# A pad of 224 bytes, GpSimd's order written out, and the first down operands loaded ahead, in a one-layer hybrid decoder block

## The chip, the cores and the metric

The kernel runs on one core of one Trainium2 chip. The metric is the device time of one execution in microseconds (us). Beside it stands the span of one profiled execution, from its first to its last instruction. The engines are TensorE (PE: matmuls and transposes; PEld: its weight loads), VectorE (DVE), ScalarE (ACT) and GpSimd (POOL); SP (SyncE) only issues the DMAs, in its own order.

## The reference

One layer over 1024 tokens of width 1024, in float32, cut to what matters here:

```python
h = rmsnorm(x, g_attn); proj = h @ w_in            # two mixers read it
mix = concat(dilated_attention(...), diff_attention(...))
x = x + mix @ w_out                                # (1024,1024) @ (1024,1024)
h = rmsnorm(x, g_ffn)
gate, up = split(h @ w_gate_up, 2)                 # 2 x 2816 columns
x = x + (silu(gate) * up) @ w_down                 # 2816 rows
return rmsnorm(x, g_final)
```

## The kernel before

Every float32 operand of a matmul is split in a high part (a cast to the matmul type, by ScalarE) and a low part (the rest, by GpSimd or VectorE); a product is then three matmuls: high by high, high by low, low by high. `split` (L684 to 687) makes such a pair, `split_weights` (L125) that of a weight tile of 1024 columns. One matmul is 128x128 by 128x512.

The stages follow each other: input projections and attention; the out projection, whose first three quarters (`op` in the profile) run among the attention heads, and whose last quarter (`op_l`, L626, rows 2 and 3 of the mixers' tiles) comes after them; the second norm; gate and up; down; the last norm.

**Around the last out projection.** Eight token tiles t go in the order 0, 2, 4, 6, 1, 3, 5, 7. For each there are two groups of six matmuls (n = 0, 1), added to `x1[t]` by VectorE (L628), and then `norm` (L153): ScalarE squares and sums (L157), VectorE scales the sum (L141), GpSimd raises it to the power -1/2 (`nst_f`, L143), and two halves of `hn_f` are written: by VectorE (L165), or, for the second half of tiles 0, 2, 4 and 6, by ScalarE (L162) and GpSimd (L163). `flip_low(j)` transposes the two halves of tile 2j on PE (`tp_b`, L846, two PSUM buffers with the tag T), and ScalarE and VectorE write them as high and low parts of the operands `h` (L848, L849). `flip_high(j)` does so for tile 2j+1 and for a difference `t` (L865). `others(j)` (L873 to 875, GpSimd) forms three more differences in place.

**Gate and up.** For pairs p = 0 to 10 of 128 columns each of gate and up is a matrix of 2x2 blocks. For p = 0 eight plain block products are used (`gate_up_first`), whose left operands `ops` are split from `raw_g` and `raw_u` (L687); for the others, seven products of sums of blocks (`pa`, `pb`, `pc`, `pd` in the profile, 12 matmuls each, L747). `store_act` splits the block results into `ao` and stores them in DRAM as `act_d[p]`.

**Down.** The seven products are run over pairs of p: `oa` (from `act_d`, L951) by `wd` (from `raw_d`, L956, differences formed by GpSimd at L968 to 974), in the order 1, 5, 6, 7, 2, 3, 4, each 24 matmuls (`d`, L1015), summed in `acc`. Three of `acc` start as `x1` read back from DRAM (`acc<-x_d`). The last p is done by plain products (`dl`, L1051), followed by the last norm (L1054 to 1067).

**What sets the order.** A scheduler orders each engine's instructions by a model of their costs; in the stretch from the last out projection to the first products of p = 1, a `manual_schedule` block keeps PE's instructions in the order of the code. All DMAs go through SP, one after the other in SP's order; each also waits until the eighth DMA before it has landed. Tiles come from pools of a fixed number of buffers, and a tile's first writer waits for the last reader of the buffer before it: `raw` one buffer, `w` four, `x1t` eight, `mix` four, `oa` ten. The operands `wd` go in turn through eight buffers that the operands `wg` and `wu` used before them. The pools of one side share one stack: the pad `end_pad` lies under all tiles of the right side (`hT`, `x1`, `mix`, `mid`).

The place of the last out weights before, and the loads of the first down operands:

```python
wo = [out_weights(2, n) for n in range(2)]                    # L877, pool "w", raw buffer shared
...
for i in ORDER:                                               # down, first pair
    oa = [load_act(p, i) for p in pair]                       # pool "down", memory of the tiles h
```

Of the kernel before, what the change touches and what calls it, by code (L numbers as in the profile page):

```python
# [71 lines left out]
def tile_hybrid_block(  # L72
# [21 lines left out]
    wp = ctx.enter_context(tc.tile_pool(name="weights", bufs=2))  # L94

    ep = ctx.enter_context(tc.tile_pool(name="end", bufs=1, side="right"))
    ep.tile([P, 24], F32, name="end_pad")
    dp = ctx.enter_context(tc.tile_pool(name="scratch", bufs=1, space=DRAM))
    pp = ctx.enter_context(tc.tile_pool(name="psum", bufs=2, space=PSUM))

# [19 lines left out]
        return bass.AP(tensor=ap1d.tensor, offset=ap1d.offset, ap=[[0, P], [1, n]])  # L120


    def split_weights(src, a, name, tag="w", eng=None):

        small = tag == "w"  # L125
        pool = wp if small else mapp
        raw = pool.tile([P, 1024], F32, tag="raw" if small else "KL", bufs=1 if small else 2, name=f"raw_{name}")
        nc.sync.dma_start(raw.rearrange("p (a b) -> p a b", a=a), src)
        if small:
            w = [pool.tile([P, 1024], F32R, tag=tag, bufs=4, name=f"w_{name}_{i}") for i in "hl"]  # L130
        else:
            both = pool.tile([P, 2, 1024], F32R, tag=tag, name=f"w_{name}")
            w = [both[:, i, :] for i in range(2)]
        nc.scalar.copy(w[0], raw)
        (eng or nc.gpsimd).tensor_tensor(w[1], raw, w[0].bitcast(F32), op=ALU.subtract)
        return [w_.rearrange("p (a b) -> p a b", a=a) for w_ in w]
# [145 lines left out]
    def run_all(gen):  # L282
        for _ in gen:
            pass
# [342 lines left out]
                i += 1  # L627
        nc.vector.tensor_tensor(x1[t][:, cols], ps, x1[t][:, cols], op=ALU.add)  # L628

    def out_weights(k0, n):  # L630
        return split_weights(w_out_v[:, k0 : k0 + 2, n * 512 : (n + 1) * 512], 2, f"o{k0}_{n}")

    def out_proj(k0, first=False):
        mix = mix_tiles(k0)
# [32 lines left out]
    def h2_tile(i):  # L667
        hB[i] = h2p.tile([P, 2, 4, 512], F32R, tag=f"h{i}", name=f"h2_{i}")

    for i in (1, 6, 7, 5, 2, 4, 3):  # L670
        if i in (4, 6):
            ops0[i == 4] = h2p.tile([P, 4, 2, 512], F32R, tag=f"h{i}", name=f"ops0_{i}")
        else:
            h2_tile(i)
# [148 lines left out]
    def store_act(p, c):  # L823
# [14 lines left out]
        for i, op in ops.items():  # L838
            nc.sync.dma_start(act_d[p][i - 1], op.bitcast(F32))

    def flip(src, i, j, name):

        cols = slice(j * P, (j + 1) * P)
        ps = psum("T", f"tp_{name}")
        for k in range(4):
            nc.tensor.transpose(ps[:, k * P : (k + 1) * P], src[:, k * P : (k + 1) * P], ident)  # L846
        pv = ps.rearrange("p (a b) -> p a b", a=4)
        nc.scalar.copy(hB[i][:, 0, :, cols], pv)  # L848
        nc.vector.tensor_tensor(  # L849
            hB[i][:, 1, :, cols], pv, hB[i][:, 0, :, cols].bitcast(F32), op=ALU.subtract  # L850
        )
# [22 lines left out]
        g.tensor_tensor(v[:, LO], u[:, LO], v[:, LO], op=ALU.add)  # L874
        g.tensor_tensor(v[:, HI], v[:, HI], v[:, LO], op=ALU.subtract)

    wo = [out_weights(2, n) for n in range(2)]  # L877
    mix = mix_tiles(2)
    load_mix(mix, 2, 0)
    gf = mid.tile([P, D], F32, tag="gf", bufs=1, name="gf")  # L880
    nc.sync.dma_start(gf, broadcast(g_ffn[0], D))
    load_mix(mix, 2, 1)
    raw0 = [load_raw(0, up) for up in range(2)]
    with tc.manual_schedule(engines={mybir.EngineType.PE}):
        for i, t in enumerate(TOKENS):
            for n in range(2):
                out_proj_group(mix, wo[n], t, n, "l")
            high = xp.tile([P, D], F32, tag="x1t", name=f"hn_f{t}") if t % 2 else None
            hns[t] = norm(mid, x1[t], gf, t, "f", high)
            nc.sync.dma_start(x1_d[t], x1[t])  # L890
            if 2 <= i < 6:
                flip_low(i - 2)
        a0 = [[], []]
        for up in range(2):
            for i in range(4):
                a0[up].append(as_left(ops0[up][:, i]))
                split(raw0[up][i], a0[up][i], nc.gpsimd)
        c0 = [block_tile(0, up) for up in range(2)]
        first = [gate_up_first(up, a0[up], c0[up], c0[0] if up else None) for up in range(2)]
        flip_high(0)  # L900
        for i in range(8):
            next(first[i // 4])
            if i % 2 == 0 and i < 6:
                flip_high(1 + i // 2)
        w1 = [gate_up_weights(1, 0)]
        for j in range(4):
            others(j)
        for i in range(4):
            next(first[0])
            flip(hns[2 * i + 1][:, LO], 7, i, f"t3_{i}")  # L910
        h2_tile(6)
        w1.append(gate_up_weights(1, 1))
        for i in range(4):
            next(first[1])
            flip(hns[2 * i][:, LO], 6, i, f"t2_{i}")
        h2_tile(4)
        store_act(0, c0[1])
        gate = block_tile(1, 0)
        steps = gate_up(1, 0, w1[0], BANK_SETS[0], gate)
        for i in range(4):  # L920
            next(steps)
            flip(hns[2 * i][:, HI], 4, i, f"t4_{i}")
        for _ in steps:
            pass
    for p in range(1, NPAIR):
        for up in range(2):
            if p == 1 and not up:
                continue
            w_ = w1[1] if p == 1 else gate_up_weights(p, up)
            c = block_tile(p, up)  # L930
            run_all(gate_up(p, up, w_, BANK_SETS[up], c, gate if up else None))
            if up:
                store_act(p, c)
            else:
                gate = c
# [9 lines left out]
    def next_bank(name):  # L945
        n_ps[0] += 1
        return psum(CYCLE[n_ps[0] % 8], name)

    def load_act(p, i):
        op = dn.tile([P, 2, 512], F32R, tag="oa", bufs=10, name=f"oa_{p}_{i}")  # L950
        nc.sync.dma_start(op.bitcast(F32), act_d[p][i - 1])  # L951
        return op

    def raw_down(p):
        raw = mxp.tile([P, 2, D], F32, tag="mix", name=f"raw_d{p}")
# [34 lines left out]
    for c0 in range(0, NPAIR - 1, 2):  # L990
        pair = (c0, c0 + 1)
        last = c0 == NPAIR - 3
        raws = [raw_down(p) for p in pair]
        for i in ORDER:
            oa = [load_act(p, i) for p in pair]
            if c0 == 0:
                if i == 5:
                    load_x1(7, 1, 1)
                    load_x1(4, 1, 0)
                    for tq in range(4):  # L1000
                        g.tensor_tensor(acc[4][:, tq], acc[4][:, tq], acc[7][:, tq], op=ALU.subtract)
                elif i == 7:
                    load_x1(2, 0, 0)
                elif i == 2:
                    load_x1(3, 0, 1)
                elif i == 3:
                    nc.sync.dma_start(gfin, broadcast(g_final, D))
            wd = [right_operand(blocks, i, p) for blocks, p in zip(raws, pair)]
            for tq in range(4):
                ps = next_bank(f"d{c0}_{i}_{tq}")  # L1010
                sl = slice(tq * P, (tq + 1) * P)
                n = 0
                for a, w in zip(oa, wd):
                    for l_, r_ in ((0, 0), (0, 1), (1, 0)):
                        mm(ps, a[:, l_, sl], w[:, r_, :], start=n == 0, stop=n == 5)  # L1015
                        n += 1
                if c0 == 0 and i in (1, 5, 6):
                    nc.scalar.copy(acc[i][:, tq], ps)
                else:
                    v.tensor_tensor(acc[i][:, tq], ps, acc[i][:, tq], op=ALU.add)  # L1020
            if last:
                if i == 6:
                    combine(v, 6, 1, 6)
                elif i == 7:
                    combine(v, 7, 6, 7)
                    combine(g, 6, 6, 5)
                    combine(v, 5, 7, 5)
                elif i == 2:
                    combine(g, 2, 1, 2)
                elif i == 3:  # L1030
                    combine(g, 3, 6, 3)
                elif i == 4:
                    combine(v, 4, 7, 4)
    raw = raw_down(NPAIR - 1)
    wl = []
    for i, src in enumerate(raw):
        wl.append(ring(f"wd{NPAIR - 1}_{i}"))
        split(src, wl[i], nc.gpsimd)
    oal = [load_act(NPAIR - 1, i + 1) for i in range(4)]
    for m, rows in ((0, (2, 3)), (1, (4, 5))):  # L1040
        for tq in range(4):
            sl = slice(tq * P, (tq + 1) * P)
            t = 2 * tq + m
            y = xp.tile([P, D], F32, tag="x1t", name=f"y_{t}")
            for n, r in enumerate(rows):
                ps = next_bank(f"dl_{t}_{n}")
                i = 0
                for k in range(2):
                    a, w = oal[2 * m + k], wl[2 * k + n]
                    for l_, r_ in ((0, 0), (0, 1), (1, 0)):  # L1050
                        mm(ps, a[:, l_, sl], w[:, r_, :], start=i == 0, stop=i == 5)  # L1051
                        i += 1
                v.tensor_tensor(y[:, n * 512 : (n + 1) * 512], ps, acc[r][:, tq], op=ALU.add)
            st = dn.tile([P, 2], F32, tag="fst", bufs=8, name=f"fst_{t}")  # L1054
            junk = mxp.tile([P, D], F32, tag="mix", name=f"sq_{t}")
            nc.scalar.activation(junk, y, AF.Square, accum_out=st[:, 0:1])
            rms_power(st, EPS, True)
            for n in range(2):
                cols = slice(n * 512, (n + 1) * 512)
# [30 lines left out]
```

## Time and profile before

| | us |
|---|---|
| median of three runs | 1272.24 |
| lowest, highest | 1271.81, 1273.27 |
| the profiled execution | 1273.28 |
| its span | 1271.5 |
| PE busy in the span | 1232.7 |
| VectorE, GpSimd, ScalarE busy | 782.0, 737.3, 578.7 |

The span is 1.8 us shorter than the profiled execution, which is 1.0 us above the median. A row of the waits reads: who waited, at which line, for whom; then the total, the number of waits and the longest. A row of the timeline reads: start, duration, engine, line, operation, output and inputs, sizes, number of instructions merged, and in brackets the idle time before it with what ended it. A row of the windows gives the stretch, then the busy time of each engine with the number of its instructions, then the clock granted to PE, the share of the DMA engines in use, and GB/s.

### The profile page before, as it was taken

The numbers are of one execution on the slowest core, as the hardware profiler recorded it, in microseconds if no ns is written. First come the engines' busy times: TensorE is split into PE (matmuls) and PEld (weight loads), VectorE is DVE, ScalarE is ACT, GpSimd is POOL, SyncE is SP. The second block draws the span as 40 slices with busy tenths as digits, with TensorE's granted clock in tenths as the row PEclk, the third lists the DMA queues.
The fourth block names the chain that finished last, engine by engine and source line by source line (L and its number), as shares of the span: only waits on it lengthen the run. The fifth ranks groups of instructions, "written<-read, shape, count | busy, mean of one in ns | idle before, by whom it ended". The sixth has DMA issues, their size and how long they took to land.

```text
span 1271.5 us, 18475 instructions
## 1 busy us (share of the span) xinstructions
PE 1232.7 (97%) x6318; PEld 1040.1 (82%) x6318; DVE 782.0 (62%) x1666; ACT 578.7 (46%) x1298; POOL 737.3 (58%) x664
## 2 busy tenths in 40 slices
PE   6999999999999999988999999999999989999997
PEld 5989989988998888867888888888888867888885
DVE  6558678876765687748555454553555543655587
ACT  5446566665765665435433334343444343222214
POOL 2024434454443444346645887878978895756676
PEclk8999999999999999998999999999999999999999
DMA  6232133123213472252332354424445359956633
GB/s 216 64 91 76 51 100 92 43 86 98 92 51 92 149 291 100 84 177 96 116 116 83 116 182 166 168 98 144 154 166 182 132 199 410 399 202 246 216 131 132
DMA packets 99613, 184.63 MB, mean 145 GB/s; under 512 B 6920, under 2 KB 58376, under 8 KB 99520
## 3 DMA queue, kind: packets, MB, share of 16 engines
q1 hardware_dynamic: 99520, 183.46, 41.6%
q8 instruction: 50, 0.82, 0.3%
q14 instruction: 43, 0.35, 0.1%
HBM read 119.41 MB, written 55.63 MB: 138 GB/s over the span
## 4 chain that ended last, share of the span: by engine, by line
PE 85%; DMA 5%; DVE 5%; POOL 2%; ACT 1%; issue 1%; SPq 0%; DVEq 0%; POOLq 0%; ACTq 0%
PE d L1015 11%; PE pa_u L747 5%; PE op L626 5%; PE pa_g L747 5%; PE pd_g L747 4%; PE pc_g L747 4%; PE pc_u L747 4%; PE pd_u L747 4%; PE vpsa L221 4%; PE ppsqa L248 4%; PE ppsqd L248 4%; PE ppskd L248 3%; PE ppska L248 3%; PE pb_g L747 3%; PE pb_u L747 3%; PE vpsd L221 3%
## 5 line engine op out<-in xcount | busy, mean ns | idle before, releaser
L1015 PE MATMUL d<-wd,oa 128*128 128x512 f32 x840 | 197.4, 396 | 6.3 <-DMA oa<-act_d 6.3
L1015 PEld LDWEIGHTS d<-wd,oa 128*128 128x128 f32 x840 | 158.2, 189 | 45.4 <-ACT wd L686 5.2
L1020 DVE TENSOR_TENSOR acc<-d,acc 128x512 f32<-128x512 f32 x128 | 87.2, 688 | 68.7 <-PE d L1015 68.6
L545 POOL TENSOR_SCALAR t_a<-t_a,st_a 128x384 f32<-128x384 f32 (+2 forms) x96 | 55.6, 590 | 105.9 <-DVE st_a L441 75.2
L687 POOL TENSOR_TENSOR wd<-raw_d,wd 128x512 fp32r<-128x512 f32 x54 | 73.4, 1380 | 69.4 <-ACT wd L686 66.9
L686 ACT CAST wd<-raw_d 128x512 fp32r<-128x512 f32 x74 | 45.3, 620 | 148.1 <-PE d L1015 95.0
L687 POOL TENSOR_TENSOR ao<-act,ao 128x512 fp32r<-128x512 f32 x52 | 74.7, 1445 | 47.8 <-ACT ao L686 47.5
L687 POOL TENSOR_TENSOR wu<-raw_u,wu 128x512 fp32r<-128x512 f32 x50 | 69.2, 1401 | 29.3 <-DMA act_d<-ao 18.6
L686 ACT CAST wg<-raw_g 128x512 fp32r<-128x512 f32 x70 | 42.1, 619 | 92.1 <-POOL raw_g L700 36.1
L687 POOL TENSOR_TENSOR wg<-raw_g,wg 128x512 fp32r<-128x512 f32 x50 | 74.8, 1513 | 5.3 <-ACT wg L686 2.9
L686 ACT CAST wu<-raw_u 128x512 fp32r<-128x512 f32 x70 | 40.7, 619 | 68.7 <-DMA raw_u<-in_w_gate_up 27.2
L431 ACT ACTIVATE t_d<-t_d,st_d 128x384 f32<-128x384 f32 (+3 forms) x96 | 58.5, 613 | 14.6 <-DVE st_d L418 14.1
L456 ACT CAST ath_a<-tp_a 128x384 fp32r<-128x384 f32 (+2 forms) x96 | 45.1, 479 | 42.8 <-PE tp_a L450 41.7
L431 ACT ACTIVATE t_a<-t_a,st_a 128x384 f32<-128x384 f32 (+2 forms) x96 | 58.7, 613 | 12.5 <-DVE st_a L418 11.7
L747 PE MATMUL pc_u<-h,wu 128*128 128x512 f32 x240 | 60.5, 395 | 0.0
L747 PE MATMUL pc_g<-h,wg 128*128 128x512 f32 x240 | 59.9, 391 | 0.0
L747 PE MATMUL pa_g<-h,wg 128*128 128x512 f32 x240 | 59.5, 393 | 0.3 <-ACT gate L773 0.3
L747 PE MATMUL pa_u<-h,wu 128*128 128x512 f32 x240 | 59.5, 393 | 0.0
L747 PE MATMUL pd_u<-h,wu 128*128 128x512 f32 x240 | 59.2, 392 | 0.0
L747 PE MATMUL pd_g<-h,wg 128*128 128x512 f32 x240 | 58.6, 393 | 0.0
L503 POOL TENSOR_SCALAR t_d<-t_d,st_d 128x384 f32<-128x384 f32 (+3 forms) x48 | 30.0, 634 | 47.0 <-DVE st_d L441 32.5
L686 ACT CAST ao<-act 128x512 fp32r<-128x512 f32 x74 | 42.4, 618 | 30.8 <-DVE act L760 11.4
(266 smaller groups left out, 3579.4 us busy)
## 6 DMA issues: line engine op xcount, KB each, us to landing
act_d<-ao SPq DMA_DIRECT2D x74, 512.0 KB, 3.4
oa<-act_d SPq DMA_DIRECT2D x74, 512.0 KB, 4.7
raw_g<-in_w_gate_up SPq DMA_DIRECT2D x11, 1024.0 KB, 6.2
raw_u<-in_w_gate_up SPq DMA_DIRECT2D x11, 1024.0 KB, 6.0
raw_d<-in_w_down SPq DMA_DIRECT2D x11, 1024.0 KB, 7.4
strip<-gtab SPq DMA_DIRECT2D x12, 512.0 KB, 3.7
xt<-in_x SPq DMA_DIRECT2D x8, 512.0 KB, 5.2
raw_o<-in_w_out SPq DMA_DIRECT2D x8, 512.0 KB, 3.9
```

The lines of the kernel that those rows point to most:

```text
L221: mm(ps[:, :256], l_, r_, start=n == 0, stop=n == 3 * KT - 1)
L248: mm(ps, l_[:, k, :], r_[:, k, sl], start=i == 0, stop=i == 3 * KT - 1)
L431: nc.scalar.activation(tt[:, :n], tt[:, :n], AF.Exp, bias=st[:, last : last + 1], scale=-1.0, accum_out=st[:, 2 + c : 3 + c],)
L456: nc.scalar.copy(hi, pv)
L503: nc.gpsimd.tensor_scalar(t0[:, :n], t0[:, :n], s0[:, 4:5], 1.0, op0=ALU.mult, op1=ALU.mult)
L545: nc.gpsimd.tensor_scalar(t0[:, :n], t0[:, :n], s0[:, 4:5], 1.0, op0=ALU.mult, op1=ALU.mult)
L626: mm(ps, l_[:, k, sl], r_[:, k, :], start=i == 0, stop=i == 5)
L686: nc.scalar.copy(dst[:, 0], src)
L687: eng.tensor_tensor(dst[:, 1], src, dst[:, 0].bitcast(F32), op=ALU.subtract)
L747: mm(ps, a[:, l_, k, :], b[:, r_, k, :], start=start and i == 0, stop=i == 11, skip_group_check=not start,)
L1015: mm(ps, a[:, l_, sl], w[:, r_, :], start=n == 0, stop=n == 5)
L1020: v.tensor_tensor(acc[i][:, tq], ps, acc[i][:, tq], op=ALU.add)
```

## The change

Five things are edited. The pad under the right side's tiles grows from 24 to 56 floats (224 bytes). The second half of the last out weights, high and low, goes into a tile `wo_l1` in the place of the operand tile `h7` instead of two `w` buffers, and the tile `h7` proper is made later. In the stretch of the last out projection GpSimd's instructions too keep the order of the code, and there the splits of the first gate operands stand behind the norms of tiles 6, 1, 3 and 5, those of the up operands behind all. Four loads of `act_d` (products 1 and 5 of p = 0 and 1) are made ahead of the last up block, into `x1t` buffers instead of the down stage's own. In the last norm the squares of the last tile are summed in two halves.

```diff
-    ep.tile([P, 24], F32, name="end_pad")
+    ep.tile([P, 56], F32, name="end_pad")
...
-        if small:
+        if parts:
+            w = parts
+        elif small:
             w = [pool.tile([P, 1024], F32R, tag=tag, bufs=4, name=f"w_{name}_{i}") for i in "hl"]
...
+    wo_l1 = None
     for i in (1, 6, 7, 5, 2, 4, 3):
-        if i in (4, 6):
+        if i == 7:
+            wo_l1 = h2p.tile([P, 4, 1024], F32R, tag=f"h{i}", name="wo_l1")
+        elif i in (4, 6):
...
+    def load_act(p, i, pool, tag, bufs):
+        op = pool.tile([P, 2, 512], F32R, tag=tag, bufs=bufs, name=f"oa_{p}_{i}")
+        nc.sync.dma_start(op.bitcast(F32), act_d[p][i - 1])
+        return op
...
-    wo = [out_weights(2, n) for n in range(2)]
+    wo = [out_weights(2, 0), out_weights(2, 1, [wo_l1[:, i] for i in range(2)])]
...
-    with tc.manual_schedule(engines={mybir.EngineType.PE}):
+    a0 = [[as_left(ops0[up][:, i]) for i in range(4)] for up in range(2)]
+    with tc.manual_schedule(engines={mybir.EngineType.PE, mybir.EngineType.Pool}):
         for i, t in enumerate(TOKENS):
...
             if 2 <= i < 6:
                 flip_low(i - 2)
-        a0 = [[], []]
-        for up in range(2):
-            for i in range(4):
-                a0[up].append(as_left(ops0[up][:, i]))
-                split(raw0[up][i], a0[up][i], nc.gpsimd)
+            if i >= 3 and i < 7:
+                split(raw0[0][i - 3], a0[0][i - 3], nc.gpsimd)
+        for i in range(4):
+            split(raw0[1][i], a0[1][i], nc.gpsimd)
+    with tc.manual_schedule(engines={mybir.EngineType.PE}):
...
+        h2_tile(7)
         w1 = [gate_up_weights(1, 0)]
...
             c = block_tile(p, up)
+            if up and p == NPAIR - 1:
+                early = {(q, i): load_act(q, i, xp, "x1t", 8) for i in (1, 5) for q in range(2)}
             run_all(gate_up(p, up, w_, BANK_SETS[up], c, gate if up else None))
...
-            oa = [load_act(p, i) for p in pair]
+            oa = [early.get((p, i)) or load_act(p, i, dn, "oa", 10) for p in pair]
...
+            halves = t == KT - 1
...
+                if halves:
+                    nc.scalar.activation(junk[:, cols], y[:, cols], AF.Square, accum_out=st[:, n : n + 1])
+            if halves:
+                v.tensor_tensor(st[:, 0:1], st[:, 0:1], st[:, 1:2], op=ALU.add)
+            else:
+                nc.scalar.activation(junk, y, AF.Square, accum_out=st[:, 0:1])
```

The order that comes of it differs in three places; up to the last out projection all engines keep theirs.

**First place: the norms after the last out projection.** GpSimd before, from the low part of the last out weights on (`nst_f` is the power, `hn_f` with `gf` the second half of a normalised tile, `ops_6` and `ops_4` the first gate and up operands):

```order
L135 TENSOR_TENSOR w_o_1_l<-raw_o_1_6913,w_o_1_h 128x1024
L687 TENSOR_TENSOR ops_6_6826<-raw_g_6927,ops_6_6826 128x512 x4
L143 TENSOR_TENSOR nst_f_6949<-nst_f_6949,nhalf 128x1
L687 TENSOR_TENSOR ops_4_6830<-raw_u_6929,ops_4_6830 128x512 x4
L143 TENSOR_TENSOR nst_f_6974<-nst_f_6974,nhalf 128x1
L163 TENSOR_TENSOR hn_f_6950<-hn_f_6950,gf 128x512
```

GpSimd now, from tile 6's second half on (the rows ahead of it are the powers and second halves of tiles 0, 2 and 4; L883 and L884 are `others`):

```order
L165 TENSOR_TENSOR hn_f_7037<-hn_f_7037,gf 128x512
L692 TENSOR_TENSOR ops_6_6826<-raw_g_6925,ops_6_6826 128x512
L145 TENSOR_TENSOR nst_f_7078<-nst_f_7078,nhalf 128x1
L692 TENSOR_TENSOR ops_6_6826<-raw_g_6925,ops_6_6826 128x512
L883 TENSOR_TENSOR hn_f_7077<-hn_f_7077 128x512
L884 TENSOR_TENSOR hn_f_6948<-hn_f_7077,hn_f_6948 128x512
L145 TENSOR_TENSOR nst_f_7118<-nst_f_7118,nhalf 128x1
L692 TENSOR_TENSOR ops_6_6826<-raw_g_6925,ops_6_6826 128x512
```

The eight splits that stood ahead of the first second half stand behind four of them, among the powers of the odd tiles and `others`.

**Second place: ScalarE in the same stretch.** ScalarE now, from the high part of the last out weights on (L159 squares, L164 scales a second half, L858 writes a high part of `h`):

```order
L136 CAST wo_l_6827<-raw_o_1_6913 128x1024
L159 ACTIVATE hn_f_6948,nst_f_6947<-x_0_5584 128x1024
L691 CAST ops_6_6826<-raw_g_6925 128x512 x3
L164 ACTIVATE hn_f_6948<-x_0_5584,nst_f_6947 128x512
L691 CAST ops_6_6826<-raw_g_6925 128x512
L159 ACTIVATE hn_f_6973,nst_f_6972<-x_2_5586 128x1024
L691 CAST ops_4_6830<-raw_u_6927 128x512 x4
L858 CAST h_1_6825<-tp_b_0_7006 128x4x128
L159 ACTIVATE hn_f_6998,nst_f_6997<-x_4_5588 128x1024
L858 CAST h_2_6829<-tp_b_0_7013 128x4x128
L164 ACTIVATE hn_f_6973<-x_2_5586,nst_f_6972 128x512
```

The casts of `ops` still stand among the first norms; before, all eight of them stood ahead of the first scaling (L162) and the first square stood behind four of them.

**Third place: the start of the down stage.** PE now, from the fifth product of the last up block on:

```order
L752 MATMUL pd_u_10387<-h_5_6828,wu_5_10316 128x512 x10
L1024 MATMUL d_1_0_10468<-wd_1_10462,oa_1_10324 128x512 x3
L1024 MATMUL d_1_1_10476<-wd_1_10462,oa_1_10324 128x512 x3
L1024 MATMUL d_1_0_10468<-wd_1_10465,oa_1_10326 128x512
L1024 MATMUL d_1_1_10476<-wd_1_10465,oa_1_10326 128x512
L1024 MATMUL d_1_2_10484<-wd_1_10462,oa_1_10324 128x512 x3
L1024 MATMUL d_1_2_10484<-wd_1_10465,oa_1_10326 128x512
L1024 MATMUL d_5_2_10530<-wd_5_10507,oa_5_10328 128x512
L1024 MATMUL d_1_3_10492<-wd_1_10462,oa_1_10324 128x512 x3
L752 MATMUL pc_u_10373<-h_4_7606,wu_4_10304 128x512 x12
L752 MATMUL pd_u_10387<-h_3_6831,wu_3_10320 128x512 x12
L1024 MATMUL d_1_0_10468<-wd_1_10465,oa_1_10326 128x512 x2
```

Before, the two products `pc_u` and `pd_u` of 12 followed the ten directly, and all matmuls `d` came behind them; now 16 matmuls `d` stand ahead of the two. SP's queue there now:

```order
L844 DMA act_d_3_6899<-ao_4_10144 128x1024
L848 DMA oa_1_10324<-act_d_0_6833 128x1024
L848 DMA oa_1_10326<-act_d_0_6840 128x1024
L848 DMA oa_5_10328<-act_d_4_6837 128x1024
L848 DMA oa_5_10330<-act_d_4_6844 128x1024
L844 DMA act_d_5_6901<-ao_6_10150 128x1024
L844 DMA act_d_4_6900<-ao_5_10156 128x1024
```

The four loads stood behind the first store of the last block (`act_d_0<-ao_0`) before, and now stand some ten DMAs earlier. Behind that store now come two loads of `acc`, the second store (`act_d_1<-ao_1`), and only then `oa_6`.

More of the change, by code (lines that the diff above doesn't have):

```diff
@@ L120, in broadcast, with split_weights @@
         return bass.AP(tensor=ap1d.tensor, offset=ap1d.offset, ap=[[0, P], [1, n]])
-    def split_weights(src, a, name, tag="w", eng=None):
+    def split_weights(src, a, name, tag="w", eng=None, parts=None):
         small = tag == "w"
@@ L628, in out_proj_group, with out_weights @@
         nc.vector.tensor_tensor(x1[t][:, cols], ps, x1[t][:, cols], op=ALU.add)
-    def out_weights(k0, n):
-        return split_weights(w_out_v[:, k0 : k0 + 2, n * 512 : (n + 1) * 512], 2, f"o{k0}_{n}")
+    def out_weights(k0, n, parts=None):
+        return split_weights(w_out_v[:, k0 : k0 + 2, n * 512 : (n + 1) * 512], 2, f"o{k0}_{n}", parts=parts)
     def out_proj(k0, first=False):
@@ L947, in next_bank @@
         return psum(CYCLE[n_ps[0] % 8], name)
[L949 to L952, printed above, removed]
     def raw_down(p):
@@ L1038, in tile_hybrid_block @@
         split(src, wl[i], nc.gpsimd)
-    oal = [load_act(NPAIR - 1, i + 1) for i in range(4)]
+    oal = [load_act(NPAIR - 1, i + 1, dn, "oa", 10) for i in range(4)]
     for m, rows in ((0, (2, 3)), (1, (4, 5))):
@@ L1044, in tile_hybrid_block @@
             y = xp.tile([P, D], F32, tag="x1t", name=f"y_{t}")
+            st = dn.tile([P, 2], F32, tag="fst", bufs=8, name=f"fst_{t}")
+            junk = mxp.tile([P, D], F32, tag="mix", name=f"sq_{t}")
+            halves = t == KT - 1
             for n, r in enumerate(rows):
@@ L1052, in tile_hybrid_block @@
                         i += 1
[L1053 to L1056, printed above, removed]
+                cols = slice(n * 512, (n + 1) * 512)
+                v.tensor_tensor(y[:, cols], ps, acc[r][:, tq], op=ALU.add)
+                if halves:
[4 more added lines that the diff above has]
+                nc.scalar.activation(junk, y, AF.Square, accum_out=st[:, 0:1])
             rms_power(st, EPS, True)
```

## The prediction

> **What bounds the kernel now.** I read the page's first lines, then the table of PE's waits, then windows of PE's clock, then the timelines of all engines at the two places where PE stands still.
>
> ```profile
> span 1271.5 us, 18475 instructions
> PE 1232.7 (97%) x6318; PEld 1040.1 (82%) x6318; DVE 782.0 (62%) x1666; ACT 578.7 (46%) x1298; POOL 737.3 (58%) x664
> ...
> PE d L1015 <- DMA oa<-act_d: 6.3, 4, 3.4
> ...
> PE tp_b L846 <- POOL hn_f L163: 4.6, 1, 4.6
> PE op_l L626 <- POOL w_o_l L135: 1.9, 1, 1.9
> PE tp_b L846 <- DVE hn_f L165: 1.4, 1, 1.4
> PE op_l L626 <- ACT w_o_h L134: 0.9, 1, 0.9
> ...
> 560.00:562.00 2.00, 2.00 (x5) 1.58 (x6) 0.00 (x0) 0.28 (x1) 0.00 (x0) 0.56 1.05 351
> ...
> 576.00:578.00 2.00, 2.00 (x7) 1.61 (x6) 1.87 (x2) 1.19 (x2) 2.00 (x3) 0.50 0.00 0
> ...
> 700.00:760.00 60.00, 60.00 (x263) 49.05 (x262) 27.83 (x35) 22.73 (x41) 51.65 (x38) 1.00 0.43 156
> ...
> 1042.00:1044.00 2.00, 2.00 (x7) 1.51 (x6) 2.00 (x2) 0.00 (x0) 2.00 (x2) 0.50 0.99 270
> ```
>
> PE is the bound: 1232.7 of 1271.5 us, and in the gate and up blocks 60 of every 60, with GpSimd at 52. So a wait taken from PE ahead of those blocks is time saved, unless it comes back later. The waits that the change touches are the four at the last out projection (8.8 us) and those for `oa` (6.3). After such waits PE also runs at a granted clock of 0.5 for some microseconds, so that seven matmuls fill 2 us in two of these windows.
>
> By the Trainium skill, "TensorE: Matmul & The Clock Gate", section "What's actually happening", the clock falls to half after at least one idle window of about 3.4 us. The level agrees with the 0.50 here, the length less so: the first slow window follows waits of 0.9 and 1.9 with one matmul between them.
>
> **The last out projection.** PE's six matmuls of tile 0, second half, wait for the weights; then its transposes wait for the first norm.
>
> ```profile
> 545.56 0.38 SPq L128 DMA_DIRECT2D raw_o<-in_w_out  x1
> ...
> raw_o<-in_w_out SPq DMA_DIRECT2D x8, 512.0 KB, 3.9
> ...
> 556.44 1.04 ACT L134 CAST w_o_h<-raw_o 128x1024 fp32r<-128x1024 f32 x1 [10.56 <-PE op L626]
> 561.72 2.18 ACT L686 CAST ops<-raw_g 128x512 fp32r<-128x512 f32 x4 [4.24 <-DMA raw_g<-in_w_gate_up]
> 565.80 2.18 ACT L686 CAST ops<-raw_u 128x512 fp32r<-128x512 f32 x4 [0.84 <-DMA raw_u<-in_w_gate_up]
> 576.13 0.72 ACT L162 ACTIVATE hn_f<-x,nst_f 128x512 f32<-128x512 f32 x1 [1.47 <-POOL nst_f L143]
> ...
> 557.56 2.35 POOL L135 TENSOR_TENSOR w_o_l<-raw_o,w_o_h 128x1024 fp32r<-128x1024 f32 x1 [9.89 <-ACT w_o_h L134]
> 562.42 5.07 POOL L687 TENSOR_TENSOR ops<-raw_g,ops 128x512 fp32r<-128x512 f32 x4 [2.51 <-ACT ops L686]
> 573.87 1.26 POOL L163 TENSOR_TENSOR hn_f<-hn_f,gf 128x512 f32<-128x512 f32 x1
> ...
> 589.13 1.41 DVE L165 SCALAR_TENSOR_TENSOR hn_f<-x,nst_f,gf 128x512 f32<-128x512 f32 x2
> 594.19 3.00 DVE L165 SCALAR_TENSOR_TENSOR hn_f<-x,nst_f,gf 128x512 f32<-128x512 f32 x2
> ...
> 599.11 0.66 PE L846 MATMUL tp_b<-ident,hn_f 128*128 128x128 f32 x4 [0.56 <-DVE h L849]
> ...
> 605.86 0.44 PE tp_b L846 x4
> ```
>
> The weights' place: the raw half is asked for at 545.6 and takes 3.9, yet its cast stands idle 10.56 us until PE has left the `w` buffer at 556.4. In `wo_l1` it can run at 549.5, the low part is there by 549.5 + 1.0 + 2.4 = 552.9, and PE comes at 556.4. Both waits go: 2.8 us. The cover is 3.5 us; without it they come back one for one.
>
> The norms: PE needs 0.234 us a matmul (96 of them take 22.5 us in a row quoted below), 1.4 a group of six, and 0.44 for four transposes. From 556.4 it does five groups (tiles 0, 2, 4) and is at the first transposes at 563.4. The power no longer stands behind the splits. But the new order of ScalarE keeps three casts of `ops` ahead of tile 0's scaling, and `raw_g` lands at 561.7: 561.7 + 3 x 0.55 + 0.72 + GpSimd's 1.26 = 565.4. PE does the first four transposes and waits 1.6. Tile 6's twelve matmuls end at 568.7. For tile 2 ScalarE has the four up casts ahead, which end at 565.8 + 2.2 = 568.0, then two writes of `h` (0.6 each, as the casts below, 1.14 for two), a square (1.04 in the last norm's row), a scaling (0.72): 571.0, and GpSimd's 1.26 make 572.2; without the transposes' 0.44 PE has stood 3.1 more. After tile 1 the same queue holds both PSUM buffers of the transposes once more; I take 1.7 us, between the two waits worked out. Tiles 3, 5 and 7 and the transposes between them (3 x 2.8 + 2 x 0.9, with tile 1's 2.8) then bring PE to the first `flip_high` at 572.6 + 2.8 + 0.9 + 2.8 + 0.9 + 1.7 + 5.6 = 587.3, and with some 2 us of half clock at 589.3.
>
> The eight splits do not vanish: at 1.27 each (5.07 for four) they lie where VectorE writes the odd tiles' norms. Two of these take 1.41 us at 589.1 and 3.00 at 594.2; the second pair ran beside GpSimd. The Trainium skill, "SBUF — State Buffer", section "Who interferes with whom", says a VectorE instruction with two SBUF inputs and a GpSimd one that reads SBUF block each other; that speaks against the change, and the two rows agree with it.
>
> In the new order the power of tile 3 stands behind a split and two steps of `others`, which wait for the difference that VectorE forms from tile 1. From VectorE's turn to tile 1 (about 581) I count 3.0 for the pair, 0.7 for `x1`, 0.7 for the difference, 2 x 1.3 on GpSimd, 0.6 the power: 588.6; then what lay between 594.2 and 599.1 before, 4.9: the second `flip_high` is ready near 593.5, and PE's own pace gives 589.3 + 0.9 + 2.8 = 593.0. Contention that hits the difference too would add 1.1. I take 594.1 against 599.1: **5.0 us** gained. From both sides: 2.8 if only the weights' waits go, and 8.2 if VectorE and the clock hold nothing back (587.3 + 3.7 = 591.0).
>
> **The start of the down stage.** PE stops when the last up block is done.
>
> ```profile
> 1031.51 2.95 PE L747 MATMUL pc_u<-h,wu 128*128 128x512 f32 x12
> ...
> 1040.70 4.57 PE L1015 MATMUL d<-wd,oa 128*128 128x512 f32 x12 [3.44 <-DMA oa<-act_d]
> ...
> 1054.96 22.52 PE L1015 MATMUL d<-wd,oa 128*128 128x512 f32 x96 [0.30 <-DMA oa<-act_d]
> 1079.25 11.10 PE L1015 MATMUL d<-wd,oa 128*128 128x512 f32 x47 [1.77 <-DMA oa<-act_d]
> ...
> 1025.24 0.38 SPq L956 DMA_DIRECT2D raw_d<-in_w_down  x1
> ...
> 1030.98 1.14 ACT L686 CAST wd<-raw_d 128x512 fp32r<-128x512 f32 x2 [7.35 <-DMA raw_d<-in_w_down]
> ...
> 1037.59 1.27 POOL L970 TENSOR_TENSOR raw_d<-raw_d 128x512 f32<-128x512 f32 x1
> ...
> 1035.23 1.26 DVE L760 TENSOR_TENSOR act<-act,gate 128x512 f32<-128x512 f32 x1
> 1038.83 1.80 DVE L687 TENSOR_TENSOR ao<-act,ao 128x512 fp32r<-128x512 f32 x1 [2.35 <-ACT ao L686]
> ...
> oa<-act_d SPq DMA_DIRECT2D x74, 512.0 KB, 4.7
> ...
> L1020 DVE TENSOR_TENSOR acc<-d,acc 128x512 f32<-128x512 f32 x128 | 87.2, 688 | 68.7 <-PE d L1015 68.6
> ```
>
> With products 1 and 5 loaded ahead, PE goes on at 1031.5 with 16 matmuls `d`. Their high parts need the second `raw_d`: asked for at 1025.2, cast at 1031.0 to 1032.1, while PE reaches them at 1032.9: 0.8 to 1.3 us of cover, and every microsecond beyond stops PE with `pc_u` and `pd_u` behind. Then these 24 (5.6), then the other 32 of products 1 and 5 (7.5): 1031.5 + 3.7 + 5.6 + 7.5 = 1048.3, where before product 6 began at 1055.0.
>
> A new wait stands there. `oa_6` is behind the store of `ao_1` in SP's queue. `ao_1` comes from `pc_u`, now done at 1040.8 - 2.8 = 1038.0, and VectorE first writes the low part of `wd_7`, whose cast is third in ScalarE's row behind GpSimd's difference (1037.6 + 1.3 = 1038.9, then 2 x 0.6: 1040.1). Then 1.8 for it (as `ao` in its row), 0.7 for the addition of `pc_u` (688 ns for its kind), 1.26, a cast 0.6, 1.80 for `ao_1`: 1046.3; two issues (0.3) and 4.7 to land: 1051.3. PE waits 3.0 us. The gain at product 6 is 1055.0 - 1051.3 = 3.7. The half clock I charge at 0.9, half of what the twelve matmuls at 1040.7 lost (4.6 instead of 2.8), as I can't tell whether this wait brings it on.
>
> The later wait of 1.77 I take as gone: product 4's `oa` now stands ahead of two `raw_d`, and 2 MB less are asked for in that stretch. Sum: 3.7 - 0.9 + 1.7 = **4.5 us**. Bounds: 8.4 if `oa_6` is in time (1055.0 - 1048.3 + 1.7); nothing if `oa_6` takes 8.8, the page's 4.7 and 4.1 more of queueing. By the page of the clock gate in the Trainium skill a wait of 3.0 us could stay under one window, and the sum would be 5.4.
>
> The early loads themselves: four issues on SP behind `ao_4`'s store, in the pause before the next `ao` is ready; hidden by PE's blocks, where the DMA share is 0.43.
>
> **The last norm and the pad.**
>
> ```profile
> 1265.13 1.04 ACT L1056 ACTIVATE sq<-y 128x1024 f32<-128x1024 f32 x1
> ...
> 1265.30 1.27 POOL L1062 TENSOR_TENSOR y<-y,gfin 128x512 f32<-128x512 f32 x1 [0.83 <-ACT y L1061]
> 1266.53 0.55 POOL L143 TENSOR_TENSOR fst<-fst,nhalf 128x1 f32<-128x1 f32 x1
> ...
> L1015 PE MATMUL d<-wd,oa 128*128 128x512 f32 x840 | 197.4, 396 | 6.3 <-DMA oa<-act_d 6.3
> L747 PE MATMUL pc_g<-h,wg 128*128 128x512 f32 x240 | 59.9, 391 | 0.0
> ```
>
> The square of the last tile gets shorter, but the power behind it waits for GpSimd's product of the tile before (1265.3 + 1.27), which is not moved: I take 0; at most half the square, 0.5, either way. The pad moves the right side's tiles by 128 bytes. No row shows what an address costs; the nearest are matmuls of one shape on tiles at different places, 391 and 396 ns, 1.3% apart, or 16 us of PE's 1233 either way as the far bounds. Nothing gives the shift a sign, so I take 0.
>
> **Sum.** 5.0 + 4.5 = 9.5 us. The profiled execution would go from 1273.3 (span 1271.5 to 1262.0) to 1263.8; it is 1.0 above the median, so the median from 1272.2 to **1262.7 us**.
>
> **The rivals.** (A) The forecast, 5.5 to 13.5 us gained, 1258.7 to 1266.7: 0.70. For it: no PE wait in the blocks between. (B) One of the two places gives nothing: the splits keep VectorE as late as before, or `oa_6` takes over the whole wait; 4.5 to 5 us gained, about 1267.5. For it: VectorE is busy throughout around 594; against it: it stood still at 560, waiting for the same weights. 0.13. (C) The gain comes back: GpSimd, now behind by eight splits, holds up the blocks' weights. It is at 52 of 60 there and can win back 8 us in 60, so I believe this little; no change, 1272: 0.05. (D) Slower: the pad makes PE's right-side operands dearer. It decides from 9.5 of 1233, 0.8% a matmul; at 1.3% the time is 1262.7 + 16 = 1278.7: 0.04. (E) Both upper bounds, 16.6 gained, 1255.6: 0.08. For it: the waits that I put in place of the old ones are worked out from orders alone.
>
> The range 1257.0 to 1268.5 holds nearly all of A, B's most and a little of E, some 0.82. What a measurement tells from no change is 0.2%, 2.5 us. Faster by more: A, E and 0.11 of B, 0.89; within: 0.04 of C and the rest of B, 0.06; slower: D and the rest of C, 0.05.
>
> **What would show it.** Right: no row `op_l` <- `w_o` among PE's waits; `hn_f` waits of 1.5 to 3 instead of 4.6; the second `flip_high` near 594; `d` beginning with no wait and one wait of about 3 ahead of product 6, released by `oa<-act_d`; none ahead of product 4. Wrong: matmuls longer than 0.234 in the blocks (D), PE waits between 650 and 1020 (C), or waits of `d` for `wd` at the early 16.

## The result, and the profile after

The median fell from 1272.36 us (1271.81 to 1273.27, four runs) to 1251.22 us (1250.45 to 1254.24, four runs): a ratio of 0.984, 95% interval 0.982 to 0.9855. That is 21.1 us where 9.5 were predicted, and it lies below the range. The profile after is that of the slowest of the four runs, 1254.24 us; the other three took 1250.45 to 1251.82. Here are the first lines of that profile, and the rows of PE's waits (who waited, for whom, total, times, longest) at the places that the prediction speaks of:

```profile
span 1252.5 us, 18470 instructions
PE 1219.6 (97%) x6318; PEld 1040.9 (83%) x6318; DVE 785.4 (63%) x1667; ACT 576.4 (46%) x1300; POOL 737.3 (59%) x664
...
PE tp_b L856 <- POOL hn_f L165: 4.0, 2, 2.0
PE d L1024 <- DMA oa<-act_d: 2.6, 1, 2.6
PE tp_b L856 <- DVE h L859: 2.6, 2, 1.8
```

The waits for `w_o` are gone, those for `hn_f` and for `oa` smaller: what was predicted. But PE, with as many instructions as before, is busy 13.1 us less. Work that was not edited got shorter. Where that happened shows when one follows the same matmuls through both traces. Four places of the kernel before (start, duration, then what ran):

```profile
546.72 0.40 PE L626 MATMUL op_l<-w_o_h,mixh 128*128 128x512 f32 x1
...
612.11 0.60 PE L846 MATMUL tp_b<-ident,hn_f 128*128 128x128 f32 x4
...
1029.24 2.44 PE L747 MATMUL pd_u<-h,wu 128*128 128x512 f32 x10
...
1240.79 22.30 PE L1051 MATMUL dl<-wd,oa 128*128 128x512 f32 x96
```

and the same four of the changed kernel:

```profile
543.74 0.39 PE L628 MATMUL op_l<-w_o_h,mixh 128*128 128x512 f32 x1
...
605.59 0.60 PE L856 MATMUL tp_b<-ident,hn_f 128*128 128x128 f32 x4
...
1017.88 2.43 PE L752 MATMUL pd_u<-h,wu 128*128 128x512 f32 x10
...
1220.96 21.92 PE L1063 MATMUL dl<-wd,oa 128*128 128x512 f32 x96
```

The lead is 3.0 us at the first `op_l`, although no instruction ahead of it was moved; 6.5 after the norms, so 3.5 there; 11.4 at the end of the blocks, 4.8 more in a stretch in which PE waits for the same 1.0 us in both kernels; and 19.8 at the first `dl`, 8.5 more. The windows of the blocks show where it comes from. Before, then after (stretch, PE's busy time and count of matmuls, the other engines, PE's clock, DMA share, GB/s):

```profile
700.00:1000.00 300.00, 300.00 (x1305) 245.15 (x1304) 147.90 (x183) 116.76 (x207) 253.24 (x182) 1.00 0.42 148
```

```profile
700.00:1000.00 300.00, 300.00 (x1322) 247.22 (x1321) 154.76 (x189) 118.88 (x212) 250.65 (x179) 1.00 0.42 150
```

Both have PE busy throughout at a clock of 1.00, yet 1322 matmuls fit where 1305 did: one each 226.9 ns instead of 229.9. The groups by line say the same of the down stage's matmuls (count, busy time, mean ns of one, idle time ahead of them):

```profile
L1024 PE MATMUL d<-wd,oa 128*128 128x512 f32 x840 | 192.9, 391 | 2.8 <-DMA oa<-act_d 2.6 <-ACT wd L691 0.2
...
L752 PE MATMUL pc_u<-h,wu 128*128 128x512 f32 x240 | 59.2, 389 | 0.0
```

391 ns where the row of before has 396, and `pc_u` 389; before, that row is:

```profile
L747 PE MATMUL pc_u<-h,wu 128*128 128x512 f32 x240 | 60.5, 395 | 0.0
```

Of the five edits only the pad reaches the attention and all the blocks. So the theory to test was **P**: about 12 us come from the 128 bytes by which the pad moves the right side's tiles, and the rest is what the prediction said. Its rival was **W**: the matmuls are shorter because PE pauses less, or at other times.

### The profile page after: what moved, and what is told of

Its sections match the earlier page's. It is cut to its first block, busy times and chain, and to the rows that moved or that the text cites. A ratio compares the mean times of both kernels' runs of the same rounds, so it can differ in the third digit from the quotient of the medians.

```text
span 1252.5 us, 18470 instructions
## 1 busy us (share of the span) xinstructions
PE 1219.6 (97%) x6318; PEld 1040.9 (83%) x6318; DVE 785.4 (63%) x1667; ACT 576.4 (46%) x1300; POOL 737.3 (59%) x664
## 5 line engine op out<-in xcount | busy, mean ns | idle before, releaser
L1024 PE MATMUL d<-wd,oa 128*128 128x512 f32 x840 | 192.9, 391 | 2.8 <-DMA oa<-act_d 2.6
```

## The experiments

Each kernel was timed in turns with the kernel before on the same chip. The ratios are to that kernel, with their 95% intervals. It took 1271.86 to 1272.36 us in the median in all rounds, so the medians below are compared directly.

| run | median us (lowest to highest) | ratio |
|---|---|---|
| the change | 1251.22 (1250.45 to 1254.24) | 0.984 (0.982 to 0.9855) |
| e1, before with the pad alone | 1262.37 (1260.81 to 1264.14) | 0.993 (0.991 to 0.994) |
| e2, the change with the old pad | 1262.74 (1261.43 to 1265.07) | 0.993 (0.991 to 0.994) |
| e3, old pad, left side moved instead | 1251.19 (1248.89 to 1251.57) | 0.983 (0.9815 to 0.984) |
| e4, pad of 480 bytes | 1251.13 (1249.90 to 1251.75) | 0.983 (0.982 to 0.985) |
| e5, no early loads | 1256.51 (1255.86 to 1258.87) | 0.9885 (0.987 to 0.990) |
| e6, last out projection as before | 1255.42 (1254.59 to 1256.84) | 0.987 (0.986 to 0.989) |
| e7, old place of the weights | 1252.12 (1251.13 to 1252.41) | 0.9845 (0.983 to 0.986) |
| e8, old order of GpSimd | 1253.04 (1252.20 to 1255.10) | 0.986 (0.984 to 0.987) |
| e9, product 6 loaded ahead too | 1247.01 (1245.12 to 1249.60) | 0.980 (0.979 to 0.982) |
| e10, last norm in one piece | 1251.32 (1248.80 to 1252.02) | 0.983 (0.982 to 0.984) |
| e11, pad of 160 bytes | 1260.25 (1259.36 to 1260.44) | 0.990 (0.989 to 0.992) |
| e12, pad of 192 bytes | 1263.01 (1259.91 to 1264.81) | 0.993 (0.991 to 0.994) |

### The pad by itself (e1), and the change without it (e2)

e1 is the kernel before, e2 the changed one, each with one line edited:

```diff
-    ep.tile([P, 24], F32, name="end_pad")      # e1
+    ep.tile([P, 56], F32, name="end_pad")
```
```diff
-    ep.tile([P, 56], F32, name="end_pad")      # e2
+    ep.tile([P, 24], F32, name="end_pad")
```

> The kernel before with one edit: the pad at the right end of SBUF has 224 bytes instead of 96, so that every tile of the right side lies 128 bytes lower; no engine's order changes. Theory P (the pad): in the two traces the same matmuls of the attention, whose order the change leaves alone, ran ahead by 2.7 us more at 551 us than at 100, those of the gate and up blocks by 4.8 more and those of the down stage by some 4.2 that no wait explains, about 12 us in all; these come from where the two operands of a matmul lie to one another. Then this kernel takes 1272.3 - 12 = 1260 us (1258 to 1262), and the matmuls d go from 396 ns to some 391. Rival W (the waits): the matmuls are shorter because PE pauses less or at other times; then the pad alone gives nothing, 1272 us (1271 to 1273.5).

> The changed kernel with the pad of before (96 bytes), all else of the change kept. Theory P: the 12 us come back, 1263 us (1261 to 1265), which would be the time predicted for the whole change; matmuls d at 396 ns. Rival W: 1251 us as with the whole change (1250 to 1253).

The pad alone gives 9.7 us (1272.03 to 1262.37), with not one instruction moved; taken out of the change it costs 11.5 (1251.22 to 1262.74). By the intervals of the ratios the two values can't be told apart. Rival W has fallen. The groups by line, and the window of the blocks, of e1 and then of e2:

```profile
L1015 PE MATMUL d<-wd,oa 128*128 128x512 f32 x840 | 192.8, 391 | 7.0 <-DMA oa<-act_d 7.0
...
700.00:1000.00 300.00, 300.00 (x1321) 247.08 (x1320) 153.89 (x187) 116.46 (x207) 251.99 (x180) 1.00 0.42 149
```

```profile
L1024 PE MATMUL d<-wd,oa 128*128 128x512 f32 x840 | 196.8, 396 | 2.3 <-ACT acc L1027 2.3
...
700.00:1000.00 300.00, 300.00 (x1306) 245.19 (x1305) 149.34 (x187) 117.55 (x207) 250.06 (x179) 1.00 0.41 145
```

391 ns and 1321 or 1322 matmuls with 224 bytes, 396 and 1305 or 1306 with 96, whichever kernel it is. e1 lies 0.4 us above its expected 1258 to 1262. Its waits of `d` for `oa` grew from 6.3 to 7.0; that PE now comes sooner to the same loads is a likely reason, and was not tested.

### Which side, and which distance (e3, e4, e11, e12)

By the layout, which says where each tile lies in SBUF, the two operands of 2484 of the 4088 512-column matmuls lie 128 bytes off a multiple of 256 from one another in the kernel before, and none in the changed one. e3 reaches the changed kernel's distances from the other side; e4, e11 and e12 try other distances.

```diff
-    ep.tile([P, 56], F32, name="end_pad")      # e3, the changed kernel
+    ep.tile([P, 24], F32, name="end_pad")
...
+    cp.tile([P, 32], F32, name="left_pad")
     ident = cp.tile([P, P], F32, name="ident")
```
```diff
-    ep.tile([P, 56], F32, name="end_pad")
+    ep.tile([P, 120], F32, name="end_pad")     # e4; 40 in e11, 48 in e12
```

> The changed kernel with the pad of before, and with a tile of 128 bytes that nothing uses put in front of the left side's tiles: the left tiles move up by 128 bytes instead of the right ones down. Against one another the two sides lie as in the changed kernel, but each tile begins 128 bytes past the place where it began. Theory P-relative (what counts is the distance between a matmul's two operands): 1251 us (1250 to 1253), matmuls d at 390 ns. Theory P-absolute (what counts is where a tile begins by itself): then all operands lie as the costly ones of before did, 1263 us or more, matmuls d at 396 or more. Rival W: 1251 us.

> The changed kernel with a pad of 480 bytes: the right side's tiles lie another 256 bytes lower. Theory P-256 (distances that are multiples of 256 bytes are all alike): 1251 us (1250 to 1253). Theory P-512 (the distance has to be a multiple of 512 bytes; in the changed kernel's trace the few 512-column matmuls with 256 bytes over followed after 232 ns, the others after 228): the right-side operands are dear again, 1263 us (1261 to 1265). Rival W: 1251 us.

> The changed kernel with a pad of 160 bytes: the two sides lie 64 bytes off a multiple of 256 from one another, where they lay 128 off with 96 bytes and none with 224. Theory S (any distance off a multiple of 256 costs the same): 1262.7 us (1261.5 to 1264). Theory Q (the cost grows with the distance, half as far costs half): 1257 us (1255.5 to 1258.5). Theory T (64 bytes are a multiple that is good enough): 1251 us (1250 to 1252).

> The changed kernel with a pad of 192 bytes: the two sides lie 32 bytes off a multiple of 256 from one another. Theory S: 1262.7 us (1261.5 to 1264). Theory Q: a quarter of the 11.5, 1254.1 us (1252.7 to 1255.4). Theory T: 1251 us (1250 to 1252) if 32 is good enough too; if 64 was and 32 is not, more than that.

e3 takes 1251.19: it is the distance between the two sides that counts, not where either begins. e4 takes 1251.13: 256 bytes more change nothing. 64 bytes off cost 9.0 us (e11) and 32 off 11.8 (e12), nearly as much as 128, so the cost doesn't shrink with the distance (theory S, e11 a little below its range). The row of `d` in e3, e4, e11 and e12 (the profile of e12 is of its fastest run, 3.1 us below its median):

```profile
L1024 PE MATMUL d<-wd,oa 128*128 128x512 f32 x840 | 191.9, 390 | 4.4 <-DMA oa<-act_d 3.6 <-DVE acc L1029 0.8
```
```profile
L1024 PE MATMUL d<-wd,oa 128*128 128x512 f32 x840 | 192.6, 391 | 2.7 <-ACT acc L1027 2.7
```
```profile
L1024 PE MATMUL d<-wd,oa 128*128 128x512 f32 x840 | 197.1, 397 | 2.5 <-DMA oa<-act_d 2.5
```
```profile
L1024 PE MATMUL d<-wd,oa 128*128 128x512 f32 x840 | 195.1, 394 | 2.8 <-DMA oa<-act_d 2.8
```

Set against the layout, the starts in the trace of before say which matmuls paid. Take 512-column matmuls that follow each other within 300 ns. Those with both their own and the next one's operands 128 off followed every 232.6 ns (2116 pairs), those with neither every 228.8 (1318 pairs); in e1 the same pairs take 228.0 and 227.3. With both 64 off (e11) it is 232.4 ns, with both 32 off (e12) 233.0. Over all such pairs e1 is 13.6 us shorter than before, where the two profiled runs differ by 12.5. The 256-column matmuls of the attention paid nothing: 118.7 ns before, 119.2 in e1 (640 pairs that follow within 150 ns).

A matmul's own distance is not the whole account. Of the 13.6 us, 2.0 are from the pairs with neither, and of these 1.4 are from the down stage alone: 298 pairs of `d` with no operand off take 231.6 ns before and 226.9 in e1. Outside the down stage such pairs differ by 0.5 ns (228.0 and 227.5). What made these `d` dear is open.

### The early loads (e5)

```diff
-                early = {(q, i): load_act(q, i, xp, "x1t", 8) for i in (1, 5) for q in range(2)}
+                early = {}
```

> The changed kernel without the early loads: products 1 and 5 load their left operands where they did before, in the down stage. Theory L (the loads give what the drift of the two traces leaves to the waits): from the last blocks to the last row product the changed kernel ran ahead by 8.5 us, of which 840 matmuls at 391 instead of 396 ns are 4.2; so 4.3 us come back, 1255.5 us (1254.5 to 1257), with a wait of d for oa of 3 to 4 us ahead of product 1 and another ahead of product 4. The prediction's 4.5 says the same within this. Rival H (the wait only changes its place, from product 1 to product 6, and the clock falls either way): 1251 to 1252.5.

5.3 us are lost, where theory L said 4.3; its range holds the time. In e5's timeline the waits are back ahead of product 1 and of product 4, by the rows with brackets (idle time and what ended it):

```profile
1026.69 13.96 PE L1024 MATMUL d<-wd,oa 128*128 128x512 f32 x48 [3.91 <-DMA oa<-act_d]
1041.30 22.36 PE L1024 MATMUL d<-wd,oa 128*128 128x512 f32 x96 [0.65 <-ACT acc L1027]
1065.31 9.99 PE L1024 MATMUL d<-wd,oa 128*128 128x512 f32 x43 [1.66 <-DMA oa<-act_d]
```

### The last out projection (e6, e7, e8)

e6 undoes the place of the weights and the order of GpSimd, e7 the place alone, e8 the order alone.

```diff
-    wo = [out_weights(2, 0), out_weights(2, 1, [wo_l1[:, i] for i in range(2)])]      # e6, e7
+    wo = [out_weights(2, n) for n in range(2)]
...
-    with tc.manual_schedule(engines={mybir.EngineType.PE, mybir.EngineType.Pool}):    # e6, e8
+    with tc.manual_schedule(engines={mybir.EngineType.PE}):
...
-            if i >= 3 and i < 7:
-                split(raw0[0][i - 3], a0[0][i - 3], nc.gpsimd)
-        for i in range(4):
-            split(raw0[1][i], a0[1][i], nc.gpsimd)
+        a0 = [[], []]
+        for up in range(2):
+            for i in range(4):
+                a0[up].append(as_left(ops0[up][:, i]))
+                split(raw0[up][i], a0[up][i], nc.gpsimd)
```

> The changed kernel with the last out projection as before: second half of the weights in the w buffers, GpSimd's order left to the scheduler with the splits ahead of the norms; pad and early loads kept. Theory F1 (what the drift says): 3.4 us come back, 1254.6 us (1253.5 to 1255.5), waits for w_o back with 2.8 us and one of 4 to 5 for hn_f. Theory F2 (the prediction's 5.0, with what the slow clock took after it counted as chance): 1256.2 (1255.5 to 1257.5).

> The changed kernel with the second half of the last out weights back in the w buffers, GpSimd's written order kept. Theory A (the steps add up): the weights' waits of 2.8 us come back in full, 1254.0 us (1253 to 1255). Theory B (PE waits for the norms' chain, which hangs on the landing of raw_g and ScalarE's casts and not on PE): PE comes later to the same chain, the waits for hn_f shrink from 2.0, 0.8 and 2.0 by what the weights' waits grow, and the time stays, 1251 to 1252.3.

> The changed kernel with GpSimd's order left to the scheduler again (splits ahead of the first norm), the new place of the weights kept. Theory A (the steps add up; the order is what is left of 3.4 after the place): 1251.5 to 1253, with one wait for hn_f that grows from 4.6 by what the place saves. Theory B (the place alone only moves the wait, since PE then waits 4.6 + 2.8 us for the first norm): all 3.4 us come back, 1254.6 us (1253.5 to 1256).

Both together are worth 4.2 us, between the 3.5 of the two traces and the prediction's 5.0, at the upper edge of F1. But each alone costs only 0.9 (the place) and 1.8 us (the order) when undone, and these two intervals overlap that of the whole change. The rows of the waits in e7, then in e8:

```profile
PE tp_b L854 <- DVE h L857: 2.4, 2, 2.2
...
PE op_l L628 <- POOL w_o_l L137: 1.9, 1, 1.9
...
PE tp_b L854 <- POOL hn_f L165: 1.0, 1, 1.0
PE op_l L628 <- ACT w_o_h L136: 0.9, 1, 0.9
```
```profile
PE tp_b L856 <- POOL hn_f L165: 6.6, 2, 4.0
```

In the stretch PE waits 9.5 us in e6, where both are undone, 6.2 in e7 (2.4 + 1.9 + 1.0 + 0.9), 6.8 in e8 (with 0.2 behind `h`) and 6.6 in the changed kernel (4.0 + 2.6). One of the two edits shortens the waits as much as both. The waits for the weights and those for the norms are alternatives: PE comes early and waits for `hn_f`, or comes late and finds it. That is theory B for e7. For e8 the time is nearer to A, but not for A's reason: not one wait grew, there are two, of 4.0 and 2.6. What the 0.9 and 1.8 us are, if they are more than the scatter of the runs, the waits don't show.

### The last norm in one piece (e10)

```diff
-            halves = t == KT - 1
+            halves = False
```

> The changed kernel with the last tile's norm taken in one piece again. In the changed kernel's trace the second half's square takes 0.61 us and an addition of 0.71 follows, where one square of the whole row took 1.04 before, and GpSimd's product of the tile before ends at 1247.2 either way. Theory 0 (nothing, as predicted): 1251 us within 0.5. Rival: the half square is worth what the shorter square says, 0.4 to 0.5 us slower without it, 1251.7.

0.1 us: nothing, as predicted.

### One product more ahead (e9)

The wait that stayed at the start of the down stage, in the changed kernel's timeline and in the windows behind it:

```profile
1021.91 2.56 PE L1024 MATMUL d<-wd,oa 128*128 128x512 f32 x10 [0.25 <-ACT wd L691]
1024.31 2.88 PE L752 MATMUL pc_u<-h,wu 128*128 128x512 f32 x12
1027.03 2.88 PE L752 MATMUL pd_u<-h,wu 128*128 128x512 f32 x12
1029.75 7.47 PE L1024 MATMUL d<-wd,oa 128*128 128x512 f32 x32
1039.81 20.55 PE L1024 MATMUL d<-wd,oa 128*128 128x512 f32 x83 [2.59 <-DMA oa<-act_d]
...
1040.00:1042.00 2.00, 2.00 (x5) 1.60 (x6) 2.00 (x2) 2.00 (x5) 2.00 (x2) 0.50 1.03 412
1042.00:1044.00 2.00, 2.00 (x8) 1.55 (x7) 2.00 (x2) 0.07 (x1) 2.00 (x3) 0.76 1.02 399
```

```diff
-                early = {(q, i): load_act(q, i, xp, "x1t", 8) for i in (1, 5) for q in range(2)}
+                early = {(q, i): load_act(q, i, xp, "x1t", 8) for i in (1, 5, 6) for q in range(2)}
```

> The changed kernel with the left operands of product 6 loaded ahead as well, in two more of the same free tiles, so that they no longer stand behind the store of ao_1. Theory G (the next thing to be late is the low part of wd_6): in the changed kernel's trace it is written by GpSimd from 1037.5 to 1038.8, and PE comes to it at 1037.2 + 0.2; so 1.0 to 1.4 of the 2.6 us stay as a wait for wd, and 1.2 to 2.6 us are gained with what the slow clock after the wait costs: 1249.4 us (1248.5 to 1250.2). Theory K (the wait goes whole and the clock stays up): 1247.5 us (1247 to 1248.4). Theory N (more loads at that time only push others back): 1251 to 1252.

4.2 us less than the changed kernel, 1247.01: theory K. PE's rows at the same place in e9, the group's row, and the window that had a clock of 0.50:

```profile
1023.43 2.88 PE L752 MATMUL pd_u<-h,wu 128*128 128x512 f32 x12
1026.15 26.23 PE L1024 MATMUL d<-wd,oa 128*128 128x512 f32 x115
...
L1024 PE MATMUL d<-wd,oa 128*128 128x512 f32 x840 | 190.7, 389 | 0.0
...
1040.00:1042.00 2.00, 2.00 (x10) 1.67 (x9) 0.35 (x1) 2.00 (x4) 2.00 (x2) 1.00 1.03 420
```

The 840 matmuls `d` wait for nothing (0.0), and the clock stays at 1.00. By these two traces, 2.6 us of wait and some 1.5 of slow clock (0.50 and 0.76 over 2 us each) make 4.1. But the slow clock is no fixed price of the wait. In e3 the wait is as long, and the clock stays at 1.00 behind it:

```profile
1035.90 14.34 PE L1024 MATMUL d<-wd,oa 128*128 128x512 f32 x62 [2.60 <-DMA oa<-act_d]
...
1036.00:1038.00 2.00, 2.00 (x9) 1.65 (x10) 2.00 (x2) 1.99 (x4) 2.00 (x2) 1.00 1.01 397
```

Ten traces have a wait of 2.1 to 2.9 us at this place; behind six of them the clock falls, behind four (e3, e6, e8 and e12) it doesn't. So the medians' 4.2 can't be split between wait and clock by one trace.

Theory G failed because the order that the scheduler makes differs too. In e9 GpSimd writes three low parts of `wd` in a row, ahead of product 6, which PE reaches at about 1033.4 (1026.15 and 32 matmuls of 0.227):

```profile
1027.03 5.17 POOL L692 TENSOR_TENSOR wd<-raw_d,wd 128x512 fp32r<-128x512 f32 x3
```

## Why the prediction was right, and where it was wrong

**The pad: wrong, and the whole of the miss.** The failed step is "Nothing gives the shift a sign, so I take 0". It measured 11.5 us in the change (9.7 alone). The bounds of ±16 stood there, but only their dear side became a rival (D, 0.04); the cheap side had none, though nothing spoke for the one rather than the other. With it the range would have reached well below 1257. The two rows used for the size, 391 and 396 ns, are matmuls of one shape; the prediction read them as differences between places without asking which places, and they don't sort by distance: by the layout 12 of the 240 `pc_g` and 420 of the 840 `d` have operands 128 off. The sign can be read from the trace of before where one group has both kinds: of `pd_u`, the 120 matmuls with operands 128 off take 395.4 ns, the other 120 take 389.2. The spacing says the same, 232.6 ns against 228.8. What the runs showed in place of the 0 is that the distance between the two sides' tiles has a price, paid with the pad of 96 bytes and not with that of 224.

**The rest: right in sum.** The change without the pad takes 1262.74 us (e2) where 1262.7 was predicted; 9.3 us of gain on that chip for 9.5. The nearness is in part luck, since the two terms missed in opposite directions (4.2 for 5.0, 5.3 for 4.5).

**The last out projection, 5.0 predicted, 4.2 measured (e6).** The weights' waits went. The waits of 1.6 and 3.1 us came as 2.0 and as 0.8 plus 2.0; the third, of 1.7, behind tile 1, didn't come. The second `flip_high` was put at 594.1; it started at 590.99, with 3.0 of that from the shorter attention:

```profile
562.67 0.66 PE L856 MATMUL tp_b<-ident,hn_f 128*128 128x128 f32 x4 [2.00 <-POOL hn_f L165]
...
566.85 0.63 PE L856 MATMUL tp_b<-ident,hn_f 128*128 128x128 f32 x4 [0.77 <-DVE h L859]
569.52 1.11 PE L856 MATMUL tp_b<-ident,hn_f 128*128 128x128 f32 x4 [2.04 <-POOL hn_f L165]
...
590.99 0.65 PE L856 MATMUL tp_b<-ident,hn_f 128*128 128x128 f32 x4 [1.81 <-DVE h L859]
...
592.00:594.00 2.00, 2.00 (x9) 1.58 (x8) 2.00 (x2) 1.97 (x3) 1.68 (x1) 0.60 0.00 0
594.00:596.00 2.00, 2.00 (x7) 1.59 (x6) 2.00 (x5) 0.17 (x1) 1.63 (x2) 0.55 0.00 0
```

What was not in the sum is the slow clock behind that wait: 0.60 and 0.55 over 2 us each, 1.7 us, so that 3.5 of 5.0 are left in this trace. That price too differs from trace to trace. The clock from 555 to 620 us before, in the changed kernel, and in e12, which has the same order:

```profile
555.00:620.00 65.00, 54.92 (x249) 43.77 (x248) 43.28 (x60) 31.64 (x55) 43.35 (x35) 0.92 0.40 141
...
555.00:620.00 65.00, 57.70 (x266) 46.65 (x264) 42.52 (x60) 32.75 (x58) 46.16 (x38) 0.92 0.37 136
...
555.00:620.00 65.00, 58.23 (x284) 46.99 (x283) 44.34 (x62) 32.59 (x58) 45.54 (x38) 1.00 0.39 139
```

And the sum took the weights' 2.8 us as a gain of their own, where the waits of e7 and e8 show that place and order stand in for one another. The upper bound of 8.2 should read 8.1 (599.1 less 591.0); nothing hangs on it.

**The start of the down stage, 4.5 predicted, 5.3 measured (e5).** PE ran on behind the blocks (0.25 us for `wd`); the new wait for `oa_6`, put at 3.0, was 2.59; the one ahead of product 4 went. The slow clock, put at 0.9 as half a price, cost 1.5 in this trace and nothing in e3. e5 and e9 confirm the mechanism from both sides. On the clock, the Trainium skill, "TensorE: Matmul & The Clock Gate", section "What's actually happening", asks for at least one idle window of about 3.4 us. The trace doesn't agree on the length: windows of 2 us have a mean clock of 0.50 behind a wait of 2.59, and of 0.60 behind one of 1.81.

**The last norm, 0: right** (e10).

## What to carry to other kernels

Before tuning waits on a kernel that TensorE bounds, group its matmuls by the distance in SBUF between their two operands: here 512-column matmuls whose operands lay 32, 64 or 128 bytes off a multiple of 256 from each other followed some 2% more slowly, and a pad of the right size won more (11.5 us) than all the moved work (9.3). Where an edit has bounds of both signs and nothing to choose between them, both belong in the range. When a wait remains behind a load that has been pulled ahead, pull the next load too: removing the 2.6 us that were left here gave 4.2. Look at the clock behind a wait in more than one trace before putting a price on it.

## What the runs showed of the hardware that was not expected

The spacing of 512-column matmuls on a busy PE at a clock of 1.00 depends on where the tiles of the two sides lie to one another: 228 ns with all operands at a multiple of 256 bytes from each other, 232 to 233 with both 128 off. It follows the distance between the sides, as e3 shows, and shows no grading between 32 and 128 bytes; 256-column matmuls show none of it. Why is open. No run separates the reading of the weights from that of the streamed operand; the rows of the weight loads have 188 ns for `pd_u` before and after. Nor does a run separate a matmul's own two operands from the tiles that other engines use at the time, and the dear `d` with no operand off speak for something beyond the former. The Trainium skill, "SBUF — State Buffer", section "Who interferes with whom", names the port that VectorE and GpSimd share as the only cause of contention. That rule doesn't tell of this cost: the rows of `d` here have 396 ns with one pad and 391 with the other, with every engine's order unchanged (e1).

A short wait on PE can bring on the slow clock or not: behind 2.59 us the clock fell to 0.50, behind 2.60 in e3 it stayed at 1.00.
